# Border of two layers in a hybrid decoder: where the transposes, the norm and one projection stand

## The chip, the cores and the metric

The kernel runs on one core of a Trainium2 chip. The metric is the device time of one execution in microseconds (us); three runs of the kernel before gave a median of 256.24 us. The profiled execution is one further run of the same program. TensorE (PE) multiplies, VectorE (DVE) and ScalarE (ACT) work elementwise, GpSimd (POOL) is nearly unused, and SyncE (SP) issues the loads.

## The reference

Two layers run over 256 tokens of width 1024. Each layer normalises, projects, runs three kinds of branches, and adds an output projection to the residual stream. Only what matters at the border of the layers is shown:

```python
def rms_norm(x, gain):
    xf = xf * lax.rsqrt(jnp.mean(xf * xf, axis=-1, keepdims=True) + EPS)
    return (xf * gain.astype(jnp.float32)).astype(x.dtype)

def hybrid_layer(x, ...):
    hn = rms_norm(x, norm_gain)
    proj = jnp.einsum('bsd,de->bse', hn, w_in)
    a_q, a_k, a_v, a_g, b_x, b_g, c_q, c_k, c_v, c_g = jnp.split(proj, ...)
    ...
    y = jnp.concatenate([y_a, y_b, y_c], axis=-1)
    return x + jnp.einsum('bse,ed->bsd', y, w_out)
```

After the second layer a last rms_norm with its own gain gives the output.

## The kernel before

The tokens form two tiles of 128 (t = 0, 1). The residual stream `xres` lies with tokens on partitions. For the projections the normalised input must lie with features on partitions, so it is transposed; it is then kept as a high and a low part, `xh` and `xl`. Every product of the projections is three matmuls, high x high, high x low and low x high (`mm3`, L190 to L195), so nearly all matmuls have the line L195.

Weights come in chunks of 2048 columns. `load_chunk` (L95) loads a chunk in two halves through `st` (five buffers, SP's queue); for each of four pieces ScalarE copies the high part `whi` (L103) and VectorE subtracts to get the low part `wlo` (L104). There are four buffers for `whi` and `wlo`. `weights(l, c, ahead)` (L111) asks for a chunk and for the `ahead` chunks behind it in the list; AHEAD is 2.

The order of TensorE's instructions is that of the program. The other engines' orders are set when the kernel is built, by a planner that goes by program order as priority and by when it expects each instruction to be ready. So an earlier place in the program is an earlier place in line on ScalarE, VectorE, GpSimd and SP, but not a fixed one.

At the end of a layer, the second half of the output projection runs for t = 0 and 1 and n2 = 0 and 1 (L555 to L560): twelve matmuls of 512 columns for each pair, in two halves of six, and then VectorE's addition to `xres` (L560). At the start of layer 1 (L258 to L284), for each token tile, `rms_stats` (L174) computes two Squares with their sums on ScalarE (L177), a bias `ss` on VectorE (L179), and Ln and Exp on ScalarE (L182, L184, recorded at the helper's line L82). VectorE multiplies by the result and by the gain (L264, two halves of 512 columns). TensorE transposes eight blocks of 128x128 (L267) into two banks; ScalarE copies each bank into `xh` (L187), and VectorE subtracts to get `xl` (L188). Between the tiles AV of tile 0 runs (24 matmuls of 512 columns); after tile 1's transposes come AV of tile 1 and then CV of both tiles (24 matmuls of 256 columns each). CQ, CK and the others follow.

In layer 0 the input is not transposed at the border, since it comes transposed from memory; `rms_stats` is called for both tiles there (L287), and in the end once more for both tiles (L563). GpSimd runs the small chain of `log_sigmoid_lambda` (L200 to L223) in layer 0. The softmax transposes (L431) are the other transposes of the same shape.

Of the kernel before, what the change touches and what calls it, by code (L numbers as in the profile page):

```python
# [10 lines left out]
F32R = mybir.dt.float32r  # L11
BF16 = mybir.dt.bfloat16
AF = mybir.ActivationFunctionType
ALU = mybir.AluOpType

P = 128
S = 256
D = 1024
L = 2
NT = S // P  # L20
NK = D // P
# [3 lines left out]
EPS = 1e-6  # L25
# [17 lines left out]
CH_AV, CH_CV, CH_CQ, CH_CK, CH_BX, CH_CG, CH_BG, CH_AG, CH_O = 0, 2, 3, 4, 7, 10, 11, 12, 14  # L43
# [4 lines left out]
def trunk_kernel(ctx: ExitStack, tc: tile.TileContext, x, first, wpack, prm_d, gatew, gains, consts, rope, out):  # L48
    nc = tc.nc
    act, dve, pe, gps = nc.scalar, nc.vector, nc.tensor, nc.gpsimd  # L50
# [4 lines left out]
    sb = ctx.enter_context(tc.tile_pool(name="sb", bufs=1))  # L55
    wk = ctx.enter_context(tc.tile_pool(name="wk", bufs=2))
    pp = ctx.enter_context(tc.tile_pool(name="pp", bufs=3, space=bass.MemoryType.PSUM))
    at = ctx.enter_context(tc.tile_pool(name="at", bufs=4, space=bass.MemoryType.PSUM))
    yp = ctx.enter_context(tc.tile_pool(name="yp", bufs=1, space=bass.MemoryType.PSUM))

    def bank(pool, tag):
        return pool.tile([P, 512], F32, name=tag, tag=tag)

    def scr(w):
        return wk.tile([P, 512], F32, name="scr", tag="scr", bufs=SCR)[:, 0:w]
# [15 lines left out]
    def tab(*a, **k):  # L81
        i = dep(act.activation(*a, **k), loaded["load"])  # L82
        loaded["users"].append(i)
        return i
# [7 lines left out]
    xh = sb.tile([P, NK, S], F32R, name="xh", tag="xh")  # L92
    xl = sb.tile([P, NK, S], F32R, name="xl", tag="xl")

    def load_chunk(l, c):  # L95
        hi = wsp.tile([P, 2048], F32R, name="whi", tag="whi")
        lo = wsp.tile([P, 2048], F32R, name="wlo", tag="wlo")
        for i in range(2):
            st = wst.tile([P, 1024], F32, name="st", tag="st")
            nc.sync.dma_start(out=st, in_=wpack[l, c][:, i * 1024:(i + 1) * 1024])  # L100
            for j in range(0, 1024, 512):
                ws, ss = slice(i * 1024 + j, i * 1024 + j + 512), slice(j, j + 512)
                act.activation(hi[:, ws], st[:, ss], AF.Copy)  # L103
                dve.tensor_sub(lo[:, ws], st[:, ss], hi[:, ws].bitcast(F32))  # L104
        return hi, lo
# [5 lines left out]
    def weights(l, c, ahead=AHEAD):  # L111
        last = order.index((l, c)) + ahead
        while pending and order.index(pending[0]) <= last:
            i = pending.pop(0)
            ready[i] = load_chunk(*i)
        return ready.pop((l, c))
# [10 lines left out]
    av_ps = [bank(at, "s") for _ in range(NT)]  # L127
# [5 lines left out]
    for k in range(NK):  # L133
# [7 lines left out]
        hi, lo = [a[:, o:o + 768] for a in pair]  # L141
# [16 lines left out]
    xres = cst.tile([P, NT, D], F32, name="xres")  # L158
# [3 lines left out]
    ident = con[:, C_ID:C_ID + P]  # L162
# [11 lines left out]
    def rms_stats(t):  # L174
        sq = wk.tile([P, 2], F32, name="sq", tag="sq", bufs=2)
        for i in range(2):
            act.activation(scr(512), xres[:, t, i * 512:(i + 1) * 512], AF.Square, accum_out=sq[:, i:i + 1])  # L177
        ss = wk.tile([P, 1], F32, name="ss", tag="ss", bufs=2)
        dve.tensor_scalar(ss, sq[:, 0:1], 1.0 / D, EPS, ALU.mult, ALU.add)  # L179
        ln = wk.tile([P, 1], F32, name="lnv", tag="lnv", bufs=2)  # L180
        tab(ln, sq[:, 1:2], AF.Ln, bias=ss, scale=1.0 / D)
        rstd = wk.tile([P, 1], F32, name="rstd", tag="rstd", bufs=4)  # L182
        tab(rstd, ln, AF.Exp, scale=-0.5)
        return rstd  # L184

    def split_psum(ps, hi, lo):
        act.activation(hi, ps, AF.Copy)  # L187
        dve.tensor_sub(lo, ps, hi.bitcast(F32))  # L188

    def mm3(ps, lhs, rhs, ks, first, last):  # L190
        lh, ll = lhs
        rh, rl = rhs
        seq = [(a, b, k) for a, b in ((lh, rh), (lh, rl), (ll, rh)) for k in ks]
        for i, (a, b, k) in enumerate(seq):
            pe.matmul(ps, a(k), b(k), start=first and i == 0, stop=last and i == len(seq) - 1)  # L195

    c8 = cst.tile([P, L * 2], F32, name="c8")
    nc8 = cst.tile([P, L * 2], F32, name="nc8")
# [29 lines left out]
    gn = cst.tile([P, D], F32, name="gn", tag="gn")  # L228

    for l in range(L):  # L230
        prm = prm_t[:, l * SM_P:(l + 1) * SM_P].rearrange("p (b j) -> p b j", b=2)
        if l > 0:
            xh = sb.tile([P, NK, S], F32R, name="xh", tag="xh")
            xl = sb.tile([P, NK, S], F32R, name="xl", tag="xl")
        yh = sb.tile([P, NK, S], F32R, name="yh", tag="yh")
        yl = sb.tile([P, NK, S], F32R, name="yl", tag="yl")

        def proj_a(ps, w, t, kb, nk, cw, first, last):
            v = [a.rearrange("p (k c) -> p k c", c=cw) for a in w]
            ts_ = slice(t * P, t * P + P)  # L240
            mm3(ps, [lambda k, a=a: a[:, kb + k, ts_] for a in (xh, xl)],
                [lambda k, a=a: a[:, k, :] for a in v], range(nk), first, last)

        def proj_b(c, mid=None):
            ps = bank(pp, "pp")
            v = [a.rearrange("p (k c) -> p k c", c=256) for a in weights(l, c)]
            for b in range(2):
                mm3(ps[:, b * 256:(b + 1) * 256],
                    [lambda k, a=a: a[:, k, b * P:(b + 1) * P] for a in v],
                    [lambda k, a=a: a[:, k, :] for a in (xh, xl)], range(NK), True, True)  # L250
                if b == 0 and mid:
                    mid()
            return ps
# [2 lines left out]
            return v2(ps, b), rb.rearrange("p (o t) -> p o t", o=1).broadcast_to([P, b, S])  # L256

        if l > 0:  # L258
            for t in range(NT):
                rstd = rms_stats(t)  # L260
                for half in range(2):
                    xn = scr(512)
                    cs = slice(half * 512, half * 512 + 512)
                    dve.scalar_tensor_tensor(xn, xres[:, t, cs], rstd, gn[:, cs], ALU.mult, ALU.mult)  # L264
                    tp = bank(at, "s")
                    for j in range(4):
                        pe.transpose(tp[:, j * P:(j + 1) * P], xn[:, j * P:(j + 1) * P], ident)  # L267
                    ks = slice(half * 4, half * 4 + 4)
                    split_psum(tp.rearrange("p (k c) -> p k c", k=4),
                               xh[:, ks, t * P:(t + 1) * P], xl[:, ks, t * P:(t + 1) * P])  # L270
                if t == 0:
                    av_w = [weights(l, CH_AV + i) for i in range(2)]
                    av_ps = [bank(at, "s")]
                    for i in range(2):
                        proj_a(av_ps[0], av_w[i], 0, 4 * i, 4, 512, i == 0, i == 1)

            cv_w = weights(l, CH_CV)
            cv_ps = bank(pp, "pp")
            av_ps.append(bank(at, "s"))
            for i in range(2):  # L280
                proj_a(av_ps[1], av_w[i], 1, 4 * i, 4, 512, i == 0, i == 1)
            for t in range(NT):
                proj_a(cv_ps[:, t * 256:(t + 1) * 256], cv_w, t, 0, 8, 256, True, True)
            cv_bk = [cv_ps[:, t * 256:(t + 1) * 256] for t in range(NT)]  # L284

        if l == 0:
            rstd0 = [rms_stats(t) for t in range(NT)]  # L287
# [247 lines left out]
        def out_mm(ps, w, t, half, ks, first, last):  # L535
            v = [a.rearrange("p (k c) -> p k c", c=512) for a in w]
            ts_ = slice(t * P, t * P + P)
            mm3(ps, [lambda k, a=a: a[:, 4 * half + k, ts_] for a in (yh, yl)],
                [lambda k, a=a: a[:, k, :] for a in v], ks, first, last)
# [13 lines left out]
        nc.sync.dma_start(out=gn if l == 0 else gf, in_=gains[l:l + 1, :].broadcast_to([P, D]))  # L553
        ow = [weights(l, CH_O + 2 + n2) for n2 in range(2)]
        for t in range(NT):  # L555
            for n2 in range(2):
                cs = slice(n2 * 512, n2 * 512 + 512)
                for ks in ((0, 1), (2, 3)):
                    out_mm(o_ps[t, n2], ow[n2], t, 1, ks, False, ks[0] == 2)
                dve.tensor_add(xres[:, t, cs], o_ps[t, n2], xres[:, t, cs])  # L560

    for t in range(NT):
        rstd = rms_stats(t)  # L563
        for half in range(2):
            cs = slice(half * 512, half * 512 + 512)
            ot = scr(512)
            dve.tensor_mul(ot, xres[:, t, cs], gf[:, cs])
            if half == 0:
                dve.tensor_scalar(ot, ot, rstd, None, ALU.mult)
            else:  # L570
                act.activation(ot, ot, AF.Copy, scale=rstd)
            nc.sync.dma_start(out=out[t * P:(t + 1) * P, cs], in_=ot)
# [108 lines left out]
```

## Time and profile before

| | us |
|---|---|
| median of three runs | 256.24 (256.11 to 256.57) |
| profiled execution | 255.86 |
| its span, first to last instruction | 254.1 |
| TensorE busy | 244.1 (96%) |
| VectorE busy | 191.4 (75%) |
| ScalarE busy | 165.0 (65%) |
| GpSimd busy | 11.2 (4%) |

A busy TensorE is not TensorE at its peak: matmuls overlap, so the pitch from one start to the next says more than the duration. A timeline row merges instructions of one group: start, the time from the first start to the last end, engine, line, operation, tiles and count; in brackets stands the idle time of the engine before it and what ended that.

### The profile page before, as it was taken

Reading aid. Unit: us, or ns where it says so; the run is one execution under the profiler, and the core shown is the slowest. Engines: PE = TensorE matmul, PEld = TensorE weight load, DVE = VectorE, ACT = ScalarE, POOL = GpSimd, SP = SyncE. Lnnn points to the kernel's source line nnn. Section 1 sums busy time; section 2 is a strip of 40 time slices with the busy share of each in tenths; the row PEclk is TensorE's granted clock in tenths of the full one; section 3 lists DMA queues with packets and bytes.
Section 4 is the critical chain, followed back from the end, with each engine's and each line's share of the span. In section 5 each row is a group of like instructions: output and inputs, shape, how many; then the busy total and the mean of one; then the engine's idle time right before and its main releaser. Section 6 shows DMA issues by size and latency. Waiting matters only on the chain.

```text
span 254.1 us, 4707 instructions
## 1 busy us (share of the span) xinstructions
PE 244.1 (96%) x1771; PEld 221.7 (87%) x1771; DVE 191.4 (75%) x430; ACT 165.0 (65%) x355; POOL 11.2 (4%) x29
## 2 busy tenths in 40 slices
PE   6899999999999999999999999999999999999990
PEld 2689999998999989878877999999899998987870
DVE  4674799999999579986785545499999846984253
ACT  3769878942956948975755465593495596794143
POOL 1285000000000000000000000000000000000000
PEclk9999999999999999999999999999999999999996
DMA  6999997934357550268275665531734732000022
GB/s 191 380 284 398 374 309 259 324 115 165 106 179 244 180 165 3 92 215 260 97 232 181 234 227 206 165 110 57 222 112 142 228 128 84 3 0 0 3 83 83
DMA packets 12983, 43.44 MB, mean 171 GB/s; under 512 B 1569, under 2 KB 1953, under 8 KB 12961
## 3 DMA queue, kind: packets, MB, share of 16 engines
q1 hardware_dynamic: 12672, 42.87, 50.2%
q10 hardware_dynamic: 288, 0.28, 0.4%
q8 instruction: 14, 0.23, 0.4%
q14 instruction: 9, 0.07, 0.1%
HBM read 42.09 MB, written 1.05 MB: 170 GB/s over the span
## 4 chain that ended last, share of the span: by engine, by line
PE 92%; ACT 3%; DMA 2%; SPq 0%; DVE 0%; issue 0%
PE pp L195 65%; PE s L195 8%; PE s L154 4%; PE y L341 3%; PE s L409 2%; DMA st<-first 2%; PE s L431 2%; PE pp L154 2%; PE s L382 1%; PE pp L457 1%; ACT whi L103 1%; PE s L355 1%; ACT scr L177 1%; PE s L267 0%; PE s L362 0%; PE s L380 0%
## 5 line engine op out<-in xcount | busy, mean ns | idle before, releaser
L104 DVE TENSOR_TENSOR wlo<-st,whi 128x512 fp32r<-128x512 f32 x132 | 84.8, 685 | 21.1 <-ACT whi L103 19.9
L103 ACT ACTIVATE whi<-st 128x512 fp32r<-128x512 f32 x132 | 74.9, 623 | 25.3 <-PE pp L195 10.8
L195 PE MATMUL pp<-xh,whi 128*128 128x256 f32 x352 | 50.3, 286 | 0.0
L195 PE MATMUL pp<-xl,whi 128*128 128x256 f32 x352 | 49.4, 283 | 0.0
L195 PE MATMUL pp<-xh,wlo 128*128 128x256 f32 x352 | 49.4, 283 | 0.0
L195 PEld LDWEIGHTS pp<-xh,whi 128*128 128x128 f32 x352 | 45.8, 191 | 1.4 <-issue 1.3
L195 PEld LDWEIGHTS pp<-xh,wlo 128*128 128x128 f32 x352 | 45.4, 192 | 0.0
L195 PEld LDWEIGHTS pp<-xl,whi 128*128 128x128 f32 x352 | 45.4, 192 | 0.0
L82 ACT ACTIVATE pr<-scr,mn 128x128 f32<-128x128 f32 (+1 forms) x32 | 14.1, 442 | 9.3 <-DVE mn L417 9.3
L177 ACT ACTIVATE scr<-xres 128x512 f32<-128x512 f32 x12 | 7.5, 626 | 13.2 <-DVE xres L560 13.0
L195 PE MATMUL pp<-whi,yh 128*128 128x512 f32 x48 | 14.1, 394 | 0.0
L195 PE MATMUL pp<-wlo,yh 128*128 128x512 f32 x48 | 13.8, 390 | 0.0
L195 PE MATMUL pp<-whi,yl 128*128 128x512 f32 x48 | 13.8, 390 | 0.0
L329 ACT ACTIVATE yh<-scr 128x512 fp32r<-128x512 f32 x8 | 5.0, 630 | 12.0 <-DVE scr L328 11.9
L76 ACT ACT_TABLE_LOAD x9 | 11.5, 1283 | 1.8 <-PEq L674 1.6
L82 ACT ACTIVATE scr<-scr 128x384 f32<-128x384 f32 (+1 forms) x20 | 10.8, 540 | 0.3
L195 PEld LDWEIGHTS pp<-wlo,yh 128*128 128x128 f32 x48 | 9.0, 188 | 1.9
L195 PEld LDWEIGHTS pp<-whi,yl 128*128 128x128 f32 x48 | 9.0, 188 | 1.9
L417 DVE CUSTOM_DVE_ANT_0 scr<-s,con 128x128 f32<-128x128 f32 (+1 forms) x32 | 10.2, 349 | 0.0
L195 PEld LDWEIGHTS pp<-whi,yh 128*128 128x128 f32 x48 | 8.7, 188 | 1.6
L422 DVE TENSOR_SCALAR pr<-pr,den 128x128 f32<-128x128 f32 (+1 forms) x32 | 8.7, 314 | 0.0
L560 DVE TENSOR_TENSOR xres<-pp,xres 128x512 f32<-128x512 f32 x6 | 4.1, 689 | 5.4 <-PE pp L195 5.3
(158 smaller groups left out, 348.6 us busy)
## 6 DMA issues: line engine op xcount, KB each, us to landing
st<-w_pack SPq DMA_DIRECT2D x66, 512.0 KB, 4.8
st<-first SPq DMA_DIRECT2D x7, 512.0 KB, 6.3
xres<-x_in SPq DMA_DIRECT2D x2, 512.0 KB, 7.3
out<-scr SPq DMA_DIRECT2D x4, 256.0 KB, 2.2
gw_t<-gate_w SPq DMA_DIRECT2D x2, 256.0 KB, 5.9
gn<-gains SPq DMA_DIRECT2D x1, 512.0 KB, 7.6
gf<-gains SPq DMA_DIRECT2D x1, 512.0 KB, 5.8
st<-first ACTq DMA_DIRECT2D x1, 256.0 KB, 3.3
```

Of the source, the lines that this page charges most:

```text
L76: load = act.preload_act_table_set(name)
L82: i = dep(act.activation(*a, **k), loaded["load"])
L103: act.activation(hi[:, ws], st[:, ss], AF.Copy)
L104: dve.tensor_sub(lo[:, ws], st[:, ss], hi[:, ws].bitcast(F32))
L154: pe.matmul(ps[t][:, 0:c.stop - c.start], a[:, k, t * P:(t + 1) * P], b[:, c], start=k == 0 and i == 0, stop=k == NK - 1 and i == 2)
L177: act.activation(scr(512), xres[:, t, i * 512:(i + 1) * 512], AF.Square, accum_out=sq[:, i:i + 1])
L195: pe.matmul(ps, a(k), b(k), start=first and i == 0, stop=last and i == len(seq) - 1)
L341: pe.matmul(y[hr, p * 128 + o:p * 128 + 256], vt[:, s0, hs], wts[i][:, ws], start=s0 == 0, stop=s0 == 1)
L409: pe.matmul(sps[h][:, cs], qT[h0][hr, hb, t * P:(t + 1) * P], kT[h0][hr, hb, 0:(t + 1) * P], start=True, stop=True)
L417: dve.tensor_tensor_reduce(xs[:, cs], sps[h][:, cs], nmask[:, cs], -0.125, 3e38, ALU.add, ALU.min, mn[:, t:t + 1])
L422: dve.tensor_scalar(pr[:, cs], pr[:, cs], den[:, t:t + 1], None, ALU.mult)
L431: pe.transpose(tp[:, i * P:(i + 1) * P], prob[h0 + h][:, j * P:(j + 1) * P], ident)
```

## The change

Tile 0's norm for layer 1 (`normed(0)`) is written ahead of the output groups of t = 1, and its transposes and splits (`turn`) between the two halves of the last output group. Tile 1's norm (`normed(1)`) is written ahead of the request for the CV weights, and the chunk behind CV is no longer asked for there. TensorE's order then is AV of tile 0, tile 1's transposes, CV of tile 0, AV of tile 1, CV of tile 1. The bias `ss` of every norm runs on GpSimd.

```diff
@@ rms_stats
-        dve.tensor_scalar(ss, sq[:, 0:1], 1.0 / D, EPS, ALU.mult, ALU.add)
+        gps.tensor_scalar(ss, sq[:, 0:1], 1.0 / D, EPS, ALU.mult, ALU.add)
@@ after mm3
+    def normed(t):
+        rstd = rms_stats(t)
+        xns = []
+        for half in range(2):
+            xn = scr(512)
+            cs = slice(half * 512, half * 512 + 512)
+            dve.scalar_tensor_tensor(xn, xres[:, t, cs], rstd, gn[:, cs], ALU.mult, ALU.mult)
+            xns.append(xn)
+        return xns
+
+    def turn(xns, t, hi, lo):
+        for half, xn in enumerate(xns):
+            tp = bank(at, "s")
+            for j in range(4):
+                pe.transpose(tp[:, j * P:(j + 1) * P], xn[:, j * P:(j + 1) * P], ident)
+            ks = slice(half * 4, half * 4 + 4)
+            split_psum(tp.rearrange("p (k c) -> p k c", k=4),
+                       hi[:, ks, t * P:(t + 1) * P], lo[:, ks, t * P:(t + 1) * P])
@@ start of a layer
-            xh = sb.tile([P, NK, S], F32R, name="xh", tag="xh")
-            xl = sb.tile([P, NK, S], F32R, name="xl", tag="xl")
+            xh, xl = next_x
@@ if l > 0
+            xn1 = normed(1)
+            av_w = [weights(l, CH_AV + i, 1 - i) for i in range(2)]
+            cv_w = weights(l, CH_CV, 0)
+            av_ps, cv_ps = [], bank(pp, "pp")
             for t in range(NT):
-                rstd = rms_stats(t)
-                for half in range(2):
...
+                av_ps.append(bank(at, "s"))
+                for i in range(2):
+                    proj_a(av_ps[t], av_w[i], t, 4 * i, 4, 512, i == 0, i == 1)
                 if t == 0:
-                    av_w = [weights(l, CH_AV + i) for i in range(2)]
-                    av_ps = [bank(at, "s")]
-                    for i in range(2):
-                        proj_a(av_ps[0], av_w[i], 0, 4 * i, 4, 512, i == 0, i == 1)
-
-            cv_w = weights(l, CH_CV)
-            cv_ps = bank(pp, "pp")
-            av_ps.append(bank(at, "s"))
-            for i in range(2):
-                proj_a(av_ps[1], av_w[i], 1, 4 * i, 4, 512, i == 0, i == 1)
-            for t in range(NT):
+                    turn(xn1, 1, xh, xl)
                 proj_a(cv_ps[:, t * 256:(t + 1) * 256], cv_w, t, 0, 8, 256, True, True)
@@ end of a layer, second half of the output projection
         for t in range(NT):
+            if t == 1 and l == 0:
+                next_x = [sb.tile([P, NK, S], F32R, name=n, tag=n) for n in ("xh", "xl")]
+                xn0 = normed(0)
             for n2 in range(2):
                 cs = slice(n2 * 512, n2 * 512 + 512)
                 for ks in ((0, 1), (2, 3)):
                     out_mm(o_ps[t, n2], ow[n2], t, 1, ks, False, ks[0] == 2)
+                    if (l, t, n2, ks[0]) == (0, 1, 1, 0):
+                        turn(xn0, 0, *next_x)
                 dve.tensor_add(xres[:, t, cs], o_ps[t, n2], xres[:, t, cs])
```

## Rows read from the trace of the kernel before

**Rows 1.** The page, busy time and share of each engine.

```profile
PE 244.1 (96%) x1771; PEld 221.7 (87%) x1771; DVE 191.4 (75%) x430; ACT 165.0 (65%) x355; POOL 11.2 (4%) x29
```

**Rows 2.** TensorE's waits in the whole span: waiter, releaser, total, times, longest.

```profile
PE s L195 <- ACT xh L187: 0.3, 1, 0.3
```

**Rows 3.** Chain that ended last, border: start us, us, what.

```profile
140.12 20.15 PE pp L195 x168
```

**Rows 4.** Timeline of TensorE, border; a row's start, length, line, tiles, count.

```profile
124.67 0.62 PE L195 MATMUL s<-whi,yh 128*128 128x512 f32 x2
...
126.03 1.03 PE L267 MATMUL s<-con,scr 128*128 128x128 f32 x8
127.40 1.19 PE L195 MATMUL s<-whi,xh 128*128 128x512 f32 x4 [0.33 <-ACT xh L187]
...
132.08 1.07 PE L195 MATMUL s<-whi,xl 128*128 128x512 f32 x4
...
134.39 1.20 PE L195 MATMUL s<-whi,xh 128*128 128x512 f32 x4
135.42 1.07 PE L195 MATMUL s<-wlo,xh 128*128 128x512 f32 x4
...
139.96 1.12 PE L195 MATMUL pp<-whi,xh 128*128 128x256 f32 x8
```

**Rows 5.** Timeline of TensorE, softmax transposes of layer 0.

```profile
103.96 1.47 PE L431 MATMUL s<-con,pr 128*128 128x128 f32 x12
105.19 1.18 PE L195 MATMUL pp<-whi,yh 128*128 128x512 f32 x4
106.20 1.08 PE L195 MATMUL pp<-wlo,yh 128*128 128x512 f32 x4
```

**Rows 6.** Timeline of VectorE, border.

```profile
122.89 1.42 DVE L264 SCALAR_TENSOR_TENSOR scr<-xres,rstd,gn 128x512 f32<-128x512 f32 x2 [1.41 <-ACT rstd L82]
...
131.44 0.14 DVE L179 TENSOR_SCALAR ss<-sq 128x1 f32<-128x1 f32 x1
132.24 1.42 DVE L264 SCALAR_TENSOR_TENSOR scr<-xres,rstd,gn 128x512 f32<-128x512 f32 x2 [0.66 <-ACT rstd L82]
```

**Rows 7.** Timeline of ScalarE, border.

```profile
123.51 2.20 ACT L103 ACTIVATE whi<-st 128x512 fp32r<-128x512 f32 x4 [0.65 <-PE pp L195]
...
126.77 1.07 ACT L187 ACTIVATE xh<-s 128x512 fp32r<-128x512 f32 x2
...
131.68 0.30 ACT L82 ACTIVATE lnv<-sq,ss 128x1 f32<-128x1 f32 x1 [1.67 <-DVE ss L179]
```

**Rows 8.** The page, costliest groups: line engine op | busy us, mean ns.

```profile
L177 ACT ACTIVATE scr<-xres 128x512 f32<-128x512 f32 x12 | 7.5, 626 | 13.2 <-DVE xres L560 13.0
...
L560 DVE TENSOR_TENSOR xres<-pp,xres 128x512 f32<-128x512 f32 x6 | 4.1, 689 | 5.4 <-PE pp L195 5.3
```

**Rows 9.** Timeline of GpSimd, layer 0.

```profile
11.57 0.99 POOL L212 TENSOR_TENSOR ls<-ls,ls 128x4 f32<-128x4 f32 x1 [0.48 <-DVE ls L211]
...
18.02 0.20 POOL L217 TENSOR_TENSOR ls<-ls,ls 128x4 f32<-128x4 f32 x1
...
19.20 0.73 POOL L217 TENSOR_TENSOR ls<-ls,ls 128x4 f32<-128x4 f32 x1
...
22.72 0.22 POOL L223 TENSOR_SCALAR nc<-c 128x4 f32<-128x4 f32 x1
```

**Rows 10.** Timeline of VectorE, layer 0.

```profile
19.18 2.50 DVE L104 TENSOR_TENSOR wlo<-st,whi 128x512 fp32r<-128x512 f32 x4 [1.61 <-ACT whi L103]
```

**Rows 11.** Timeline of ScalarE, layer 0.

```profile
22.46 0.29 ACT L82 ACTIVATE lnv<-sq,ss 128x1 f32<-128x1 f32 x1
...
26.37 5.01 ACT L103 ACTIVATE whi<-st 128x512 fp32r<-128x512 f32 x8
```

**Rows 12.** Timeline of TensorE, layer 0, start of CK.

```profile
29.49 1.12 PE L195 MATMUL pp<-xh,whi 128*128 128x256 f32 x8
```

**Rows 13.** Timeline of SP's queue, border.

```profile
133.68 0.33 SPq L553 DMA_DIRECT2D gf<-gains  x1
```

More of the change, by code (lines that the diff above doesn't have):

```diff
@@ L258, in trunk_kernel @@
         if l > 0:
+            xn1 = normed(1)
+            av_w = [weights(l, CH_AV + i, 1 - i) for i in range(2)]
+            cv_w = weights(l, CH_CV, 0)
+            av_ps, cv_ps = [], bank(pp, "pp")
             for t in range(NT):
-                rstd = rms_stats(t)
-                for half in range(2):
[L262 to L270, printed above, removed]
-                if t == 0:
-                    av_w = [weights(l, CH_AV + i) for i in range(2)]
-                    av_ps = [bank(at, "s")]
-                    for i in range(2):
-                        proj_a(av_ps[0], av_w[i], 0, 4 * i, 4, 512, i == 0, i == 1)
-            cv_w = weights(l, CH_CV)
-            cv_ps = bank(pp, "pp")
-            av_ps.append(bank(at, "s"))
-            for i in range(2):
-                proj_a(av_ps[1], av_w[i], 1, 4 * i, 4, 512, i == 0, i == 1)
-            for t in range(NT):
+                av_ps.append(bank(at, "s"))
+                for i in range(2):
+                    proj_a(av_ps[t], av_w[i], t, 4 * i, 4, 512, i == 0, i == 1)
+                if t == 0:
+                    turn(xn1, 1, xh, xl)
                 proj_a(cv_ps[:, t * 256:(t + 1) * 256], cv_w, t, 0, 8, 256, True, True)
```

## Prediction

> **What bounds the kernel now.** I read the page's busy table first. TensorE is busy for 96% of the span; the next engine, VectorE, for 75% [rows 1]. So only time taken off TensorE's own line of work, or a new wait put into it, can move the end. The list of TensorE's waits over the whole span holds, after the opening, a single row: 0.3 us in front of a matmul that reads xh, released by ScalarE's copy at L187 [rows 2]. Read alone, that row makes the border of the layers worth 0.3 us. The chain that ended last runs through TensorE behind the border, in one piece of 168 matmuls [rows 3], so time saved ahead of it is saved. TensorE's timeline gives the size, because there one can compare the pitch (start to start) of its groups. Twenty matmuls of 512 columns start between 135.42 and 139.96: 0.227 us each. Measured against that pitch [rows 4]:
> - First border block (transposes of token tile 0): they start at 126.03, the next matmul at 127.40, which is 1.37 us; the following 20 matmuls take 4.68 where 20 x 0.227 = 4.54, so 0.14 more. Together 1.51 us.
> - Second block (tile 1): the last four matmuls before it start at 132.08 and fill 0.91, to 132.99; the next matmul starts at 134.39: 1.40 us. The four after it take 1.03 instead of 0.91, another 0.12. Together 1.52 us.
>
> So TensorE spends 3.03 us on 16 transposes. What they cost in a stream with nothing to wait for is seen at the softmax transposes of layer 0 (L431): twelve start at 103.96, the next matmul at 105.19, 0.1025 us each, and the four matmuls behind them take 1.01 instead of 0.91, 0.10 more [rows 5]. Eight therefore cost 0.82 + 0.10 = 0.92 us, and two blocks 1.84 us. The border holds 3.03 - 1.84 = 1.19 us that can be taken away, and no more.
> The Trainium skill, "Trainium Kernel Development and Optimization", section Performance Expectations, calls matmul busy time a bad metric for the distance to the limit, since matmuls are pipelined. The trace agrees: by the wait row the gain would be 0.3 us, by the pitch it is 1.19.
>
> **The first block, part by part.** The change puts tile 0's eight transposes between the halves of the last output group (t = 1, n2 = 1). The second half starts at 124.67 [rows 4]. What they need is the normalised tile: VectorE's two products start at 122.89 and end at 124.31 [rows 6]. Their inputs and their place ahead of the last additions are as before, so I keep these times. The first four transposes need the first product only (done near 123.6); the next four start 0.41 later, at 125.08, with 0.77 us to spare. The block ends at 124.67 + 0.92 = 125.59; then the six remaining output matmuls (1.36 us) run, and the first AV matmul can start at 126.95 instead of 127.40.
> These six matmuls now cover the copy into xh. The first four transposes are complete near 125.3. On ScalarE the split of the CV weights (four pieces, 123.51 to 125.71) may stand ahead, a copy pair takes 1.07 [rows 7], so one copy is done near 126.3 and 0.6 us is left. If a Square (0.63 [rows 8]) also stands ahead, the copy ends at 126.9, just in time; if one more weight piece does, 0.5 us is lost. VectorE's half (xl) is first read by the ninth matmul, 1.8 us later, and is no limit.
>
> **The second block.** In the old order VectorE's small bias operation (L179) came out of a full queue, with no idle ahead of it, at 131.44; ScalarE's Ln waited 1.67 us for it and the two products came at 132.24 to 133.66, too late for transposes that could have gone at 132.99 [rows 6, 7]. Now the norm of tile 1 comes before the weight splits. The last addition can follow the last output matmul, near 127.2, and take 0.7; the Square and the read of its sum take about 0.8 [rows 8]; from Ln to the first product 0.56 (131.68 to 132.24); the products 1.42. That is 130.7. If ScalarE and VectorE each have one or two weight pieces under way at the handoffs (0.5 to 0.6 each, up to 1.7 in all), it is 132.4. AV of tile 0 runs from 126.95 for 24 x 0.227 = 5.45 us, to 132.40. So the transposes do not wait, at worst barely. After them comes not AV of tile 1, which needs their result, but CV of tile 0: 24 matmuls at 0.120 us (20.15 us for 168 [rows 3]), 2.88 us. That covers the pair of copies into xh (1.07) and most of the pair into xl, which is read only later. Without this cover 0.5 us would be lost, as now.
> CV is only cut in two and reordered; its matmuls and AV's are unchanged in number, so they cost nothing more. Its weights are split by 125.71 in the trace of before [rows 7], at worst a few us later now, and are wanted at 133.3.
>
> **The bias on GpSimd.** Six operations of about 0.15 us leave VectorE [rows 6] and run on GpSimd. The trace shows none of this shape there; the nearest rows, 128x4, take from 0.20 to 0.99 us [rows 9]. They are short while VectorE is idle (0.20 at 18.02) and long once it subtracts weights (0.73 at 19.20): VectorE idled 1.61 us up to 19.18 and was then busy for 2.50 [rows 9, 10]. At the border VectorE is busy, so I take 0.7. Each bias is ready one Square and one addition before Ln wants it: at the border and at the end of the kernel over 2 us, so it costs nothing; without that slack it would cost 0.55 each time (0.7 - 0.15). The exception is layer 0, where the Squares follow each other and GpSimd is busy with the lambda chain until 22.94 [rows 9]. If the bias stands behind that chain, Ln goes not at 22.46 but up to 1.5 later (22.94 + 0.99 + the handoff). Behind Ln on ScalarE stand eight weight pieces from 26.37 (0.63 each) [rows 11]; the fourth is done at 28.9 and is wanted by CK's seventh matmul at 29.49 + 6 x 0.12 = 30.2 [rows 12], so 1.3 us is spare. Cost: nothing, at most 0.2 us.
> The Trainium skill, "GPSIMD Engine Reference", section 4.1 Engine selection, speaks against this edit: elementwise work belongs on VectorE. The trace agrees as far as one instruction goes (0.20 to 0.99 against 0.15). If each bias of the border stood on the path, the sum would be 2 x 0.55 = 1.1 us higher, 256.15; with the slack above it is 255.05.
>
> **Loads.** The loads for layer 1's CQ chunk are asked for later in the program (two DMAs, four ScalarE and four VectorE pieces). SP's queue issues the load of the final gain at 133.68, right after the last product of the norm has released its buffer at 133.66 [rows 6, 13]. That product comes earlier now, so nothing in this queue waits longer. The slot for these weights comes free with the last output matmul, and CQ starts near 144.5: ample room.
>
> **Sum.** Gain 1.19 us. New order: 126.95 + 5.45 + 0.92 + 2.88 + 5.45 + 2.88 = 144.53; before, CV ended at 139.96 + 48 x 0.12 = 145.72. Behind this TensorE shows no wait, and the weight slots are released by TensorE itself, so the whole gain should reach the end. The profiled execution took 255.86 us (span 254.1 and 1.76 around it): 254.67. The median of the runs is 0.38 above the profiled one: 256.24 - 1.19 = 255.05 us.
>
> **Rivals.**
> - The copy into xh comes late on ScalarE: a Square and a fifth weight piece ahead of it, or the products of tile 1 slip behind weight subtractions. Price 0.4 to 0.8 us, time 255.4 to 255.9. For it: the four weight pieces from 123.51 fill ScalarE just when the copy is wanted [rows 7]. Against: the copy stands ahead of them in the program. Chance 0.16.
> - The GpSimd bias is on the path. Rows of one shape range over a factor of five, and the long ones fall where VectorE subtracts [rows 9, 10]; if tile 1's bias waited until VectorE pauses, near 131, its products would end near 133.1, 0.7 us late: 255.75. Against: the slack is over 2 us, the longest row 0.99. Chance 0.03. The Trainium skill, "GPSIMD Engine Reference", section Specifications, states such a contention of GpSimd with VectorE instructions that have two SBUF inputs; the two rows at 18.02 and 19.20 agree.
> - The gain is given back downstream (a load or a weight piece that does not move forward with TensorE), or the order stays as before in effect: 256.0 to 256.4. Against: no TensorE wait after the border. Chance 0.08.
> - Slower: the in-group transposes block the output matmuls queued behind them. One mechanism: VectorE takes an addition (0.6) and the four CV weight subtractions (2.5) before the products of tile 0. Then the second product ends near 127.4 instead of 124.31, 2.3 us after the transposes want it, and the net is 1.1 slower: 257.4. It turns to slower than measurable once the product ends after about 126.8. Against: the subtractions need ScalarE's pieces, first ready near 124.1. Chance 0.09.
>
> **How the numbers follow.** Forecast 0.64: 255.05, with own range 254.7 (blocks at 0.82 without the 0.10, and a run 0.13 under the median) to 255.5. The range to 256.1 takes in the first two rivals and part of the third. A measurement can tell about 0.2%, 0.5 us: faster means under 255.73. Faster: 0.64 and about half of the first rival, 0.72; within: 0.18; slower: 0.10.
>
> **What would show it.** Right: eight transposes between two halves of the last output group, at 0.1 us pitch; no TensorE idle before the first AV matmul; CV matmuls directly after the second block; the bias on GpSimd done before Ln. Wrong: a TensorE wait on the tile-0 products or on L187's successor, or an Ln that waits for GpSimd.

## The result

Eight runs of the changed kernel have a median of 255.02 us (253.46 to 255.57), eight of the kernel before 256.26 us (255.95 to 256.57). The comparison of the runs gives a ratio of 0.9938 with a 95% interval of 0.9923 to 0.9953, so the change is faster by 0.5 to 0.8%. The profiled execution took 255.37 us with a span of 253.6.

The medians differ by 1.24 us, where 1.19 was forecast. The ratio says more, 256.26 x 0.9938 = 254.67 us, because it weighs three runs of 253.46, 253.92 and 254.20 that the median passes over (the means of the two sets of eight differ by 1.56 us); 254.67 lies 0.03 under the lower end of the range. The experiments below keep apart what goes into the two readings: the border of the layers, and what differs from run to run. Two slow runs, one of 615.57 us (of the kernel with tile 0's transposes late) and one of 1358.47 (of the kernel before), stand in no median below.

The page of the changed kernel first, busy time and share of the span:

```profile
span 253.6 us, 4715 instructions
PE 245.1 (97%) x1771; PEld 223.7 (88%) x1771; DVE 190.3 (75%) x424; ACT 164.2 (65%) x355; POOL 12.9 (5%) x35
```

Against [rows 1] hardly anything moved; VectorE has six instructions less, GpSimd six more. The border shows in TensorE's timeline (start, length, line, tiles, count), to be read against [rows 4]:

```profile
124.88 0.62 PE L195 MATMUL s<-whi,yl 128*128 128x512 f32 x2
125.33 1.03 PE L211 MATMUL s<-con,scr 128*128 128x128 f32 x8
126.12 0.72 PE L195 MATMUL s<-whi,yh 128*128 128x512 f32 x2
126.68 0.62 PE L195 MATMUL s<-wlo,yh 128*128 128x512 f32 x2
127.14 0.63 PE L195 MATMUL s<-whi,yl 128*128 128x512 f32 x2
127.60 1.08 PE L195 MATMUL s<-whi,xh 128*128 128x512 f32 x4
...
132.15 1.07 PE L195 MATMUL s<-whi,xl 128*128 128x512 f32 x4
133.06 1.03 PE L211 MATMUL s<-con,scr 128*128 128x128 f32 x8
133.85 1.20 PE L195 MATMUL pp<-whi,xh 128*128 128x256 f32 x8
134.88 1.12 PE L195 MATMUL pp<-wlo,xh 128*128 128x256 f32 x8
...
136.80 1.09 PE L195 MATMUL s<-whi,xh 128*128 128x512 f32 x4
137.73 1.07 PE L195 MATMUL s<-wlo,xh 128*128 128x512 f32 x4
```

No row carries a wait any more. The transposes (now L211) start at 125.33 and the output matmuls go on at 126.12, 0.79 us for eight; the six matmuls behind them take 1.48 instead of 1.36. First block: 0.79 + 0.12 = 0.91 us, where 0.92 was worked out (0.82 + 0.10). AV takes 5.46 (127.60 to 133.06). The second block takes 0.79, and the eight matmuls of CV behind it 1.03 instead of 0.96: 0.86 us. Both blocks together cost 1.77 us against 3.03 in [rows 4], 1.26 less.

To compare kernels I take four starts on TensorE from each trace: CQ of layer 0, the second half of the output projection of layer 0, CQ of layer 1, and the last matmul. "Border" is from the second to the third. Differences are taken before rounding.

| profile of | CQ, layer 0 | to output half | border | from CQ, layer 1, to the last matmul |
|---|---|---|---|---|
| kernel before | 23.73 | 91.42 | 30.57 | 101.62 |
| changed kernel | 24.40 | 91.41 | 29.33 | 101.62 |

The border gives 1.23 us, 0.03 less than the two blocks: AV of tile 0 takes 0.01 more than worked out, and the four matmuls behind CV of tile 0 take 0.93 (136.80 to 137.73) instead of 0.91. The stretches around it are the same to 0.02 us. What the profiles' spans don't show of it (254.1 against 253.6) was lost ahead of everything, in the opening: CQ starts 0.68 us later.

ScalarE and VectorE at the border of the changed kernel, against [rows 6, 7]:

```profile
124.17 1.68 ACT L103 ACTIVATE whi<-st 128x512 fp32r<-128x512 f32 x3 [0.58 <-PE pp L195]
125.75 0.62 ACT L177 ACTIVATE scr<-xres 128x512 f32<-128x512 f32 x1
126.27 0.19 ACT L177 ACTIVATION_READ_ACCUMULATOR scr<-xres 128x1 f32 x1
126.36 1.06 ACT L187 ACTIVATE xh<-s 128x512 fp32r<-128x512 f32 x2
...
130.54 0.28 ACT L82 ACTIVATE lnv<-sq,ss 128x1 f32<-128x1 f32 x1
```

```profile
129.15 2.50 DVE L104 TENSOR_TENSOR wlo<-st,whi 128x512 fp32r<-128x512 f32 x4
131.55 1.41 DVE L203 SCALAR_TENSOR_TENSOR scr<-xres,rstd,gn 128x512 f32<-128x512 f32 x2
```

Three weight pieces and a Square stand ahead of the copy into xh, so a Square took the place of the fourth weight piece; the first of the pair is done near 126.9 and is wanted at 127.60. The products of tile 1 come out of a full queue at 131.55 and end at 132.96. The transposes start at 133.06, and the last four, which alone need the second product, near 133.5 (0.1 us each), 0.5 us after its end. Ln has no wait. On GpSimd:

```profile
121.40 0.19 POOL L179 TENSOR_SCALAR ss<-sq 128x1 f32<-128x1 f32 x1 [96.15 <-ACT scr L177]
126.61 0.88 POOL L179 TENSOR_SCALAR ss<-sq 128x1 f32<-128x1 f32 x1 [5.02 <-ACT scr L177]
```

The first started while VectorE was idle (until 121.45), the second ran while it subtracted weights (125.55 to 127.44). Ln came 3.0 us after the second one.

### The profile page after: what moved, and what is told of

It reads as the page before. It is cut to its first block, busy times and chain, and to the rows that moved or that the text cites. A ratio compares the mean times of both kernels' runs of the same rounds, so it can differ in the third digit from the quotient of the medians.

```text
span 253.6 us, 4715 instructions
## 1 busy us (share of the span) xinstructions
PE 245.1 (97%) x1771; PEld 223.7 (88%) x1771; DVE 190.3 (75%) x424; ACT 164.2 (65%) x355; POOL 12.9 (5%) x35
## 3 DMA queue, kind: packets, MB, share of 16 engines
HBM read 42.09 MB, written 1.05 MB: 170 GB/s over the span
## 4 chain that ended last, share of the span: by engine, by line
PE 95%; DMA 1%; ACT 1%; DVE 0%; issue 0%; SPq 0%; ACTq 0%
PE pp L195 65%; PE s L195 9%; PE s L154 5%; PE y L345 3%; PE pp L154 2%; PE s L413 2%; PE s L435 2%; PE s L386 1%; PE pp L461 1%; DMA st<-first 1%; PE s L359 1%; PE s L211 1%; PE s L366 0%; PE s L384 0%; PE s L362 0%; ACT scr L177 0%
## 5 line engine op out<-in xcount | busy, mean ns | idle before, releaser
L179 POOL TENSOR_SCALAR ss<-sq 128x1 f32<-128x1 f32 x6 | 1.8, 306 | 221.0 <-ACT scr L177 220.9
```

## The experiments

The theory: the border is 1.23 us shorter in every execution, because each block of transposes has lost its wait; what else differs between runs is the opening. The rivals are that the move to GpSimd brings part of the gain, that one of the edits at the border does nothing, or that something outside the border gained too. The two edits of the bias, AV ahead of CV and the repeat of the changed kernel ran on one chip, the others on a second one, where the unedited changed kernel was not run; the kernel before had 256.30 us on the first and 256.29 and 256.36 on the second.

**The bias alone on GpSimd**, in the kernel before:

```diff
-        dve.tensor_scalar(ss, sq[:, 0:1], 1.0 / D, EPS, ALU.mult, ALU.add)
+        gps.tensor_scalar(ss, sq[:, 0:1], 1.0 / D, EPS, ALU.mult, ALU.add)
```

> The kernel before with one edit: the bias of every norm on GpSimd. Theory (the bias is off the path, and the gain of the whole change is the border's 1.23 us): 256.1 to 256.4 us, no difference to the kernel before within 0.15 us; at the border ScalarE's Ln of the second tile no longer waits for a bias that came out of VectorE's full queue, so the second block of transposes may start up to 0.3 us earlier, no more. Rival (the change gains outside the border too, 0.3 to 0.4 us of it through the bias in layer 0, since the measured 254.7 is 0.35 under the 255.05 of the sum): 255.8 to 255.9.

Measured: 256.56 us median of 12 runs beside 256.30 for the kernel before; ratio 1.0007 (0.9986 to 1.0027). The median lies 0.16 above the expected range, less than the interval can tell; it is far from the rival. Border 30.51, so 0.06 shorter. TensorE's timeline shows where the 0.06 come from and why it is no more:

```profile
128.07 1.20 PE L195 MATMUL s<-whi,xh 128*128 128x512 f32 x4 [0.33 <-ACT xh L187]
...
133.66 1.03 PE L267 MATMUL s<-con,scr 128*128 128x128 f32 x8
135.00 1.19 PE L195 MATMUL s<-whi,xh 128*128 128x512 f32 x4 [0.30 <-ACT xh L187]
```

AV of tile 0 ends at 128.07 + 5.45 + 0.14 = 133.66, and the transposes start there without the wait of before. In the kernel before, AV ended at 127.40 + 5.59 = 132.99 and the transposes started 0.06 later:

```profile
133.05 1.38 PE L267 MATMUL s<-con,scr 128*128 128x128 f32 x8
```

The next matmul stands at 134.39 there [rows 4], 1.34 us behind the start of the transposes. In this run it is 1.34 us too: what the late products cost TensorE was small, and the wait for the copy into xh stayed.

**The bias back on VectorE**, in the changed kernel (the same line the other way round).

> The changed kernel with the bias back on VectorE. Theory: the order of TensorE is the same and the bias has slack, so the border (from the first matmul of the last output groups to the first of CQ) stays at 29.33 us and the time at that of the changed kernel within 0.2 us. Rival (the move to GpSimd matters, because on VectorE the bias of tile 1 queues behind weight subtractions): the second block waits again, border 29.6 to 30.0, time 0.3 to 0.7 above the changed kernel.

Measured: 255.13 us median of 12; ratio to before 0.9961 (0.9945 to 0.9977); border 29.33. The bias runs in 0.14 us between weight subtractions, and nothing waits for it:

```profile
126.76 0.14 DVE L179 TENSOR_SCALAR ss<-sq 128x1 f32<-128x1 f32 x1
```

With the new order the engine of the bias makes no difference at the border.

**AV of both tiles ahead of CV**, in the changed kernel:

```diff
                 if t == 0:
                     turn(xn1, 1, xh, xl)
+            for t in range(NT):
                 proj_a(cv_ps[:, t * 256:(t + 1) * 256], cv_w, t, 0, 8, 256, True, True)
```

> The changed kernel with AV of both tiles ahead of CV, as in the order before: nothing runs between tile 1's transposes and the AV matmuls that read them. Theory (CV of tile 0 covers the copy into xh): the stall of the second block comes back, 1.40 + 0.12 - 0.92 = 0.5 to 0.6 us, border 29.8 to 29.95, time 0.5 to 0.6 above the changed kernel. Rival (with the norm early the copies are quick enough, so the reorder of CV is worth nothing): border 29.3 to 29.5.

Measured: border 29.91, 0.58 longer than the changed kernel's; 255.57 us median of 12, 0.4 above the changed kernel on the same chip (255.16), where 0.5 to 0.6 was expected; ratio to before 0.9977 (0.9949 to 1.0004). The wait for the copy is back:

```profile
132.44 1.03 PE L211 MATMUL s<-con,scr 128*128 128x128 f32 x8
133.77 1.19 PE L195 MATMUL s<-whi,xh 128*128 128x512 f32 x4 [0.30 <-ACT xh L187]
```

The row says 0.30, the starts say 1.33 where 0.79 would do: the tile 1 block needs the CV matmuls as cover, and they are worth 0.58 us.

**Tile 0's transposes behind the whole output group**, in the changed kernel:

```diff
-                    if (l, t, n2, ks[0]) == (0, 1, 1, 0):
-                        turn(xn0, 0, *next_x)
+                if (l, t, n2) == (0, 1, 1):
+                    turn(xn0, 0, *next_x)
```

> The changed kernel with tile 0's transposes behind the whole last output group instead of between its halves; all else as changed. Theory (the six output matmuls cover the copy into xh): the stall of the first block comes back, 1.51 - 0.92 = 0.59 us, border 29.9 us, time 0.6 above the changed kernel, about 255.7 to 255.8. Rival (the norm and the reorder gained it all, and the copy is quick now): border 29.3 to 29.5.

Measured: border 29.93, 0.59 longer; 255.64 us median of 11; ratio to before 0.9978 (0.9963 to 0.9993).

```profile
126.41 1.03 PE L211 MATMUL s<-con,scr 128*128 128x128 f32 x8
127.78 1.20 PE L195 MATMUL s<-whi,xh 128*128 128x512 f32 x4 [0.33 <-ACT xh L187]
```

This is the first block of [rows 4] again, 1.37 us from the transposes to the next matmul. Six output matmuls as cover are worth 0.59 us.

**Tile 1's norm behind the weight requests**, in the changed kernel:

```diff
-            xn1 = normed(1)
-            av_w = [weights(l, CH_AV + i, 1 - i) for i in range(2)]
-            cv_w = weights(l, CH_CV, 0)
+            av_w = [weights(l, CH_AV + i) for i in range(2)]
+            cv_w = weights(l, CH_CV)
+            xn1 = normed(1)
```

> The changed kernel with tile 1's norm written behind the requests for the AV and CV weights, and those requests again two chunks ahead. Theory of the prediction (the norm's early place brings the second block's products in time): the products come up to 1.7 us later, the second block waits 0.3 to 0.7, border 29.6 to 30.0 us. Rival, from the run with the bias alone on GpSimd, where the products ended 0.08 us ahead of the transposes although the norm stood late: the first block now starts 0.4 us earlier and no more, so the wait is under 0.2 and the border 29.3 to 29.5. Time 0 to 0.7 above the changed kernel, about 255.2 to 255.8.

Measured: border 29.59, 0.25 longer; 255.31 us median of 12; ratio to before 0.9956 (0.9936 to 0.9977). This lies at the edge of the first expectation and above the second one, so the early norm and the shorter weight requests together are worth something, though less than I had thought. TensorE and VectorE of this kernel:

```profile
133.00 1.28 PE L211 MATMUL s<-con,scr 128*128 128x128 f32 x8
134.04 1.20 PE L195 MATMUL pp<-whi,xh 128*128 128x256 f32 x8
```

```profile
129.09 3.10 DVE L104 TENSOR_TENSOR wlo<-st,whi 128x512 fp32r<-128x512 f32 x5
132.10 1.41 DVE L203 SCALAR_TENSOR_TENSOR scr<-xres,rstd,gn 128x512 f32<-128x512 f32 x2
```

Five weight subtractions stand ahead of the products instead of four. The products end at 133.51, and the transposes, which could go from 133.00 on, take 1.04 us to the next matmul instead of 0.79. The planner did not bring the norm ahead of the subtractions in either kernel. Against the start of the block, the products end 0.6 us later than in the changed kernel, one weight piece, and 0.25 of that is lost; so the changed kernel has near 0.35 us to spare. The edit also asks for weights further ahead again, and no run shows which of its two parts puts the fifth piece there.

**The changed kernel once more**, unedited, beside these on the same chip:

> The changed kernel unedited, beside the others on this chip, for its opening. In its first profile TensorE ran at half clock until 10.1 us and reached CQ of layer 0 0.6 us later than the kernel before; its runs lie between 253.5 and 255.6 where those of before lie between 256.0 and 256.6. Theory (the border gives 1.23 us in every execution and the rest is the opening, which differs from one execution to the next by when the first weights land and when the clock rises): a profile whose opening differs from the first by some tenths and whose border is again 29.33 +/- 0.05. Rival (something behind the opening differs from run to run): border or layer 1 differ by more than 0.2 us between the two profiles.

Measured: 255.16 us median of 12 (253.51 to 255.53), beside 256.30 for 35 runs of the kernel before (254.48 to 258.18); ratio 0.9963 (0.9942 to 0.9984). CQ of layer 0 at 24.08, then 91.41, border 29.33, 101.62. So the opening is the only part that differs between the two profiles of this program: their times differ by 0.33 us, their starts of CQ by 0.32. It also shows that the kernel before has low runs too; they had only not fallen into its first eight.

The opening of both profiles of the changed kernel, and of the kernel before, on TensorE. Changed kernel, first profile:

```profile
1.17 3.17 PE L131 MATMUL y<-cold 128*128 128x512 bf16 x7 [1.17 <-DVE cold L119]
5.21 1.22 PE L154 MATMUL s<-whi,xh 128*128 128x512 f32 x2 [0.87 <-ACT xh L142]
6.23 1.05 PE L154 MATMUL s<-whi,xl 128*128 128x512 f32 x2
7.08 1.05 PE L154 MATMUL s<-wlo,xh 128*128 128x512 f32 x2
...
10.64 0.62 PE L154 MATMUL s<-wlo,xh 128*128 128x512 f32 x2
11.09 0.40 PE L154 MATMUL pp<-whi,xh 128*128 128x256 f32 x2
```

Kernel before:

```profile
5.26 0.73 PE L154 MATMUL s<-whi,xh 128*128 128x512 f32 x2 [0.93 <-DVE wlo L150]
5.83 0.67 PE L154 MATMUL s<-whi,xl 128*128 128x512 f32 x2
...
8.73 0.74 PE L154 MATMUL s<-whi,xh 128*128 128x512 f32 x2 [1.05 <-ACT whi L147]
```

Between 6.23 and 7.08 two matmuls of 512 columns take 0.425 us each, from 10.64 on 0.225: TensorE ran at the lower of its two levels (1.2 GHz) and then at the upper one (2.4 GHz). The clock column of the views reads full for this stretch, so I go by the pitch. In the kernel before the upper level was there for the first weights, and TensorE then waited for the second load. Each has its own loss. Why the clock rose earlier in one than in the other, after the same warm-ups, no run shows.

**Nine warm-up matmuls instead of seven**, in the changed kernel:

```diff
-WARM = 7
+WARM = 9
```

> The changed kernel with 9 warm-up matmuls instead of 7, to test the opening, where all the difference between executions was: CQ of layer 0 starts at 23.7 to 24.5 us, later when the TensorE clock rises late (4.4 us in the profile of before, 8.7 to 10.1 in the others). Seven warm-ups end near 4.3, 0.9 before the first weights. Theory (the pause before the first weights decides when the clock rises): the clock rises before 6 us, CQ starts by 23.8, time 0.4 to 0.7 under the changed kernel, 254.5 to 254.8. Rival (the start is set by the loads of the first weights and the clock's rise by chance): CQ again 23.7 to 24.5, time 255.0 to 255.3. Border 29.33 in either case.

Measured: 254.06 us median of 5 (253.82 to 254.19), beside 256.29 of before; ratio 0.9919 (0.9900 to 0.9938); border 29.33. CQ starts at 23.18, by 23.8 as the first expectation had it; the time is 0.4 under its range. The clock did not rise before 6 us as expected: the first pair still ran at the lower level, the upper one came near 7.2. And the second load was early in this profile, ScalarE's first reader of it starting at 6.10 (the first line) against 7.96 in the first profile of the changed kernel (the second):

```profile
6.10 0.51 ACT L142 ACTIVATE xh<-st,prm_t 128x256 fp32r<-128x256 f32 x1 [0.64 <-DMA st<-first]
...
7.96 0.51 ACT L142 ACTIVATE xh<-st,prm_t 128x256 fp32r<-128x256 f32 x1 [2.81 <-DMA st<-first]
```

So the result did not tell the warm-ups from luck with the loads.

**Twelve warm-ups:**

> The changed kernel with 12 warm-up matmuls: busy from 1.2 to about 6 us. Theory of the pause: the clock has risen by the time the first weights are multiplied, which start up to 0.7 late; the loads set the pace from there, CQ by 23.7, time 254.4 to 254.8. Rival (loads and chance): the late start is added, CQ at 24.4 or later, time 255.2 to 255.8. Border 29.33 in either case.

Measured: 254.82 us median of 8 (253.89 to 255.40); ratio 0.9949 (0.9926 to 0.9971); border 29.33. The first weights' matmuls start at 5.72 and soon run at the upper level, then TensorE waits 0.77 us for the second load, and CQ starts at 23.93:

```profile
8.94 0.73 PE L154 MATMUL s<-whi,xh 128*128 128x512 f32 x2 [0.77 <-ACT whi L147]
```

The theory of the pause had CQ by 23.7, its rival at 24.4 or later: neither came; the time lies 0.02 above the first range. In this profile the clock was quick and the load set the pace.

**Nine in both kernels, and ten**, on one chip:

> The kernel before with 9 warm-up matmuls instead of 7 and nothing else. Theory (opening and border add up and have nothing to do with each other): border 30.57 as before, the stretches behind the opening and behind the border 91.4 and 101.6 us as in every profile so far, time lower than the kernel before by what the changed kernel gained from nine (255.16 to 254.06 us, 1.1): about 255.2 us. Rival (the changed kernel with nine was lucky with its loads, whose second one landed at 6.1 us in its profile against 7.4 to 8.0 in most others): 255.8 to 256.3 us.

> The changed kernel with 9 warm-up matmuls once more, beside the kernel before with nine, since its first result rests on five runs. Theory (nine shorten the opening in most executions): 254.0 to 254.4 us, border 29.33; difference to the kernel before with nine 1.1 to 1.3 us. Rival (luck with the loads): 254.8 to 255.2 us.

> The changed kernel with 10 warm-up matmuls, between 9 (254.06 us) and 12 (254.82 us). Theory (the first weights must not wait for warm-ups, and the pause before them must be short): 254.1 to 254.6 us. Rival (only the landing of the second load counts): 254.8 to 255.2, as with seven.

Measured, beside 256.36 us of the kernel before with seven (21 runs): the kernel before with nine 256.01 us median of 12, ratio 0.9984 (0.9965 to 1.0003), border 30.57; the changed kernel with nine 254.54 us, median of 7 (253.97 to 255.06), ratio 0.9936 (0.9912 to 0.9959), border 29.33; with ten 254.26 us, median of 11 (253.32 to 255.56), ratio 0.9929 (0.9904 to 0.9953), border 29.33. Two more warm-ups gave the kernel before 0.35 us by the medians (by the interval, between 0.9 and nothing), not the 1.1 that I had expected from the first result. The changed kernel with nine lies between the two expectations, with ten inside the first one, and the difference between the kernels with nine (256.01 and 254.54) is 1.47, a little above what was expected. The profile of the changed kernel with nine has the second load as late as most (7.75), TensorE at the upper level from 6.0 on, and CQ at 24.04; the first one with nine had the load early, a later clock, and CQ at 23.18. Here the landing of the second load was worth more than the clock:

| profile | first reader of the second load | clock at the upper level by | CQ, layer 0 |
|---|---|---|---|
| kernel before | 7.43 | 5.8 | 23.73 |
| changed, first | 7.96 | about 10 | 24.40 |
| changed, again | 7.91 | about 9.3 | 24.08 |
| AV first | 6.40 | about 8.7 | 23.78 |
| nine, first | 6.10 | about 7.2 | 23.18 |
| nine, again | 7.75 | 6.0 | 24.04 |
| twelve | 7.64 | before 6.4 | 23.93 |

Over all profiles with the load at 7.6 to 8.0, those not in the table included, an early clock gives CQ at 23.93 to 24.13 and a late one 24.08 to 24.47, up to 0.5 apart; with the load at 6.1 it is 23.18, but with a load nearly as early (6.4) and a late clock 23.78. So both count, and no run holds one of them fixed. The medians of the changed kernel with nine or ten (254.06, 254.54, 254.26) lie under those with seven (255.02, 255.16); but the intervals of their ratios overlap with the 0.9938 and 0.9963 of seven, and those with seven ran on another chip or in an earlier comparison; that more warm-ups help is likely and not shown.

## Why the prediction was right and where it was wrong

- **The ceiling by pitch** (3.03 us for 16 transposes now, 1.84 in a free stream, 1.19 to gain): right; 1.23 in every profile of the changed order. By the wait row alone, 0.3, it would have been missed by a factor of four. It was called all that can be taken away, and was passed by 0.04. The small rest is the second block, 0.86 and not 0.92: eight transposes took 0.79 where I had put 0.82, and CV's matmuls of 256 columns behind it lost 0.07 where I had put 0.10 from matmuls of 512.
- **First block**: right. 0.91 us for the block (0.92; 0.03 less for the transposes and 0.02 more behind them all but cancel), no wait on the products, 0.7 us spare for the copy (0.6). Undone alone it costs 0.59 (0.59).
- **Second block**: the mechanism that carries it is the CV cover, 0.58 us where I had said 0.5. The late products were given too much: with the bias alone moved they came in time, and the border was only 0.06 us shorter. The early norm was given too much as well: I wrote that the products could come at 130.7 on the old time scale, 132.4 at worst. They ended at 132.96 on the new scale, where the whole border stands 0.66 later, so 132.3: the worst case of that sum. It was in time because the last four transposes, which alone need the second product, come 0.4 us behind the first. The full queue of VectorE stayed ahead of them, with one piece less.
- **The bias**: right that it is off the path, both ways (0.06 and 0.00 us). The bound of 0.20 to 0.99 held but for 0.01: 0.19 beside an idle VectorE, 0.88 beside a subtracting one. In layer 0 it ran after the lambda chain, and the stretch behind the opening stayed at 91.41.
- **Loads, and that the gain reaches the end**: right; 101.62 us behind the border in every profile.
- **What failed** is the lower end of the range. The step reads "own range 254.7 (blocks at 0.82 without the 0.10, and a run 0.13 under the median)". The term that was mis-sized is the 0.13 for how low a run falls. It came from three runs of the kernel before, 256.11 to 256.57. The runs spread far more: 254.48 to 258.18 in 35 runs of the same kernel. Of the 0.38 us between the 255.05 forecast and 254.67, the border explains 0.04, and 0.34 is how low runs fell into the two sets of eight: three of the changed kernel and none of the kernel before. That was chance as far as the runs tell: the border alone would make the ratio 0.9952, which lies just inside the interval of this comparison and inside that of the later, larger one (0.9942 to 0.9984), whose ratio of 0.9963 is 255.3 us. With a term of about 1 us for the spread the range would have begun near 254.
- **What stays open** is where the low runs come from. Their spans are short by as much as their times (251.7 for 253.46, 253.6 for 255.37), so the time lies inside the program. In the profiles the only part that moves is the opening, which puts CQ of layer 0 anywhere from 23.18 to 24.47 while the stretches behind it, the border apart, are constant to 0.05 us. That the low runs come from there too is not shown: none of the three was profiled, and 253.46 would need CQ near 22.5 (24.40 less the 1.91 us to the profiled 255.37), earlier than in any profile. The trace of before shows waits of 0.93 and 1.05 us on the first weights, so that something there could move; I left the opening out because the change does not touch it.
- **Luck**: that the median meets the forecast to 0.03 us (255.02 and 255.05) is closer than it repeats; it was 255.16 the second time.
- **The rivals**: the copy late on ScalarE, the bias on the path, the gain given back behind the border and the output matmuls blocked did not happen. Of the first one its second half came close: the products of tile 1 did stand behind weight subtractions, and one more of these would have cost 0.25 us.

## What to carry to other kernels

Price a block of transposes, or any short step between two streams on the engine that bounds the kernel, by the pitch of the matmuls on both sides against the same step in a stream without waits; idle rows show only part of it (0.3 of 1.2 us here). A step that must pass through another engine and back needs work between that does not depend on it: six matmuls of 512 columns or 24 of 256 covered a copy of two halves, each worth 0.6 us. And put the spread of the runs into the range even if the change lies elsewhere than where they differ: three runs that agree to 0.5 us do not show it.

## What the runs showed of the hardware

Eight transposes between the two halves of an open accumulation cost the same as between finished ones: 0.79 us in both blocks of the changed kernel, and 0.12 or 0.07 in the matmuls behind. Outside the opening and the border, thirteen profiles of eleven programs agreed to 0.05 us over 193 us of TensorE's work. The same GpSimd instruction of one column took 0.19 us beside an idle VectorE and 0.88 us beside one that subtracts tiles; the Trainium skill, "GPSIMD Engine Reference", section 1 Specifications, states a contention of GpSimd with VectorE instructions that have two SBUF inputs, as these subtractions do, and these two rows agree. The 0.88 is no fixed price: with the bias alone moved, the same instruction took 0.35 us beside the three subtractions at the same place, and in both runs it ended 0.05 us after the last of them (127.49 against 127.44 and 127.45). In the opening, with the same seven warm-up matmuls, the first weights were multiplied at 2.4 GHz in two profiles and at 1.2 GHz in six, by the pitch of the matmuls, and the second load's first reader started anywhere from 6.4 to 8.0 us.
